# One transformer layer on one core: the opening written as one list, with the condition spread on chip and four tiles in the first batch

## The chip, the core and the metric

The kernel runs on one core of a Trainium2 chip, as one launch. The metric is the device time of that launch in microseconds (us), the median of three runs. The engines are TensorE (PE, with its weight loads PEld), VectorE (DVE), ScalarE (ACT), GpSimd (POOL) and SyncE (SP), which here only issues DMAs. Each runs its own instructions in the order in which they were written and waits on semaphores for the others.

## The reference

One encoder layer over 1024 tokens of 1024 features, float32. Cut to what the change touches:

```python
cond = jax.nn.silu(c)                                  # c: 1 x 1024
mod = cond @ w_ada[l] + b_ada[l]                       # 1024 x 6144
sh1, sc1, g1, sh2, sc2, g2 = jnp.split(mod, 6, axis=-1)
h = modulate(rms_norm(x, norm_mix_g[l]), sh1, sc1)     # norm(x)*(1+sc1)+sh1
proj = h @ w_in[l]
q_a, k_a, v_a, qk_m, v_m, o_m, gates = jnp.split(proj, splits, axis=-1)
y_attn = axial_gqa_attention(q_a, k_a, v_a, ...)       # 8 heads of 64
y_mem = bidirectional_mlstm(qk_m, v_m, o_m, gates, ...)
x = x + g1 * (concat(y_attn, y_mem) @ w_out[l])        # then the SwiGLU FFN, then a last norm
```

## The kernel before

Features lie on the 128 partitions and tokens along the free axis, so x is eight tiles `x0` to `x7` of 128 x 1024, worked in two halves `n` of 512 tokens. Every float32 product is made of three: each operand is split into a high part (fp32r) and the rest, and `mm3` (L295 to L297) adds high x high, low x high and high x low in PSUM. For the weights ACT makes the high part `whi` and POOL the low part `wlo`; for the normed input, ACT makes `hh` and POOL (for `x0` DVE) makes `hl`.

The opening does this. `cond`, the silu of c, is loaded onto all 128 partitions. ACT squares the tiles of x, DVE and POOL add them into `ssx`, and PE sums over the partitions with a matmul of ones (`ms`). DVE and ACT turn that into the reciprocal root (`sq`). A column of the modulation is one "dot": DVE multiplies a transposed column block `ada` (128 x 1024) with `cond` and sums along the free axis; each feature tile k needs two, column 8+k (scale) and column k (shift). Then for each half DVE multiplies x by the root, ACT applies scale and shift, ACT makes `hh`, and `hl` follows. PE takes each tile k as it comes, for the first batch of three tiles of output features: k, v and the first q tile, 18 matmuls for each k.

The work after that is a list of units, `IN`: `t` are chunk units (tokens on the partitions; `t0` holds v of the memory heads and the gates, eight times 24 matmuls of 272 columns), `q` the other q tiles, `f` the tiles that go through the convolution. Each q or f unit is 48 matmuls of 512 columns.

What sets the order: a class `Clock` keeps an expected time for each engine and emits each step when that model says it is ready. So one set of costs orders all five engines' instructions, and the DMAs on SP's one queue. Attention starts when the model says that the last q tile and the gates are ready; from there `un`, the stream of the units that are left, fills the gaps that the model sees in attention and then in the memory heads. The gates' rows pass through a long chain on DVE that ends in `dexp` and a small matmul (`T`, L918).

Buffers: `ada` columns share five `big` buffers, raw weight pieces three `wst` buffers.

```python
for f in range(3):
    mm3(acc0[f][n], weights(2 * f, k, 4), (h_hi[k][:, halves(n)], h_lo[k][:, halves(n)]),
        k == 0, k == KT - 1)
    ck.pe(0.65)
...
return rope_ok[3].done and gates_ok.done and not open_sum[0]      # stops the stage ahead of attention
```

Of the kernel before, what the change touches and what calls it, by code (L numbers as in the profile page):

```python
# [11 lines left out]
F32 = mybir.dt.float32  # L12
# [8 lines left out]
P = 128  # L21
# [19 lines left out]
WARM = 6  # L41
WARM0 = 9
POOLED = (0,)
# [4 lines left out]
IN = ([("t", 0), ("q", 1), ("q", 2), ("q", 3), ("f", 0), ("f", 4), ("f", 1), ("f", 5), ("t", 2), ("f", 2), ("f", 6),  # L48
# [21 lines left out]
class Flag:  # L70
    """done: what sets it is emitted; t: when that is expected to end"""
# [12 lines left out]
class Engine:  # L84
    """An engine's instructions with their expected times."""
# [39 lines left out]
class Clock:  # L125
    """Emits instructions in the order of expected times (us), each engine's in the order in which they are ready."""
# [16 lines left out]
    def chain(self, delay, *steps, flag=None, bg=None):  # L143
        """Functions that follow one another. bg: the engine of each step; the step waits until that is idle."""
# [35 lines left out]
    def need(self, *flags):  # L180
        """What sets the flags is emitted before what follows."""
# [23 lines left out]
    def streams(self, mains, fills=(), stop=None):  # L205
        """Runs streams, the first that is ready first, until the mains have ended or stop() holds."""
# [14 lines left out]
class Stream:  # L221
    """A part of the tensor engine's work: a generator that yields the flags that its next piece needs."""
# [15 lines left out]
def layer_kernel(ctx, tc, xT, c, w_ada, vecs, cons, rope, w_f, w_t0, w_t, w_o, w_gu, w_d, out):  # L238
# [8 lines left out]
    # ---------------------------------------------------------------- constants  # L247
    both = const.tile([P, 2], F32, name="both")
# [6 lines left out]
    nc.scalar.dma_start(con, cons)  # L255
# [15 lines left out]
    # DRAM scratch  # L271
# [39 lines left out]
    def psum_open(name, tags, bufs=1):  # L311
        """tags: name -> (tag, buffers)"""
# [7 lines left out]
    class slot:  # L320
        """what frees the next tile of a tag"""
# [26 lines left out]
    with tc.manual_schedule():  # L348
# [20 lines left out]
        va = kvp.tile([P, NJ, 2, P], F32R, name="va")  # L369
        k2 = [[kvp.tile([P, S], F32R, name=f"k2{i}{g}") for i in range(2)] for g in range(2)]  # L370
# [3 lines left out]
        # ---------------------------------------------------- weights in a ring of six pieces  # L374
# [33 lines left out]
        specs = conv_w(0) + conv_w(1) + conv_w(2)  # L408
# [12 lines left out]
        def raw(shape, src, flag, arrived):  # L421
            """a transfer into the ring of three; flag: it has been used; arrived(tile, delay)"""
# [10 lines left out]
        def split(p, delay, src, shape, *before, lo=None):  # L433
            """the parts of a piece"""
# [12 lines left out]
        def piece(i):  # L447
            """a piece; its transfer, where it has one of its own"""
# [11 lines left out]
        def load_piece():  # L460
            """the next piece, once there is room for it"""
# [20 lines left out]
        psum_open("ps0", {n: ("ps0", 8) for n in ("acc", "acct", "ms", "tr", "T")}, 8)  # L482

# [32 lines left out]
        for j in (8, 0):  # L516
            ada_load(j)
# [1543 lines left out]
```

## Time and profile before

| what | value |
|---|---|
| median of three runs | 1436.59 us (1433.66 to 1437.8) |
| span of the profiled execution, first to last instruction | 1431.8 us |
| PE busy | 1310.1 us, 91% |
| DVE busy | 1075.9 us, 75% |
| POOL busy | 792.6 us, 55% |
| ACT busy | 660.6 us, 46% |

The profile is of one execution. Its own time is known only as the span; the median of the timed runs is 4.8 us above that. Busy shares are over the whole span. The stages differ: in the opening DVE is the busiest engine, in attention and behind it PE is.

### The profile page before, as it was taken

The page shows a single profiled execution, that of the slowest core. Times are in us where ns is not written, and L with a number is a line of the kernel's source. Part 1 is how long each engine was busy: PE and PEld are TensorE (multiplying, and loading weights), DVE is VectorE, ACT ScalarE, POOL GpSimd, SP SyncE. Part 2 cuts the span into 40 slices and gives each one's busy share as a digit, 9 for nine tenths or more (in the row PEclk, how much of TensorE's full clock was granted, in tenths as well). Part 3 has the DMA queues.
Part 4 walks back from the last instruction along what each step waited for, and adds up shares of the span by engine and source line. Part 5 has one row for each costly group of instructions (what it writes and reads, how often), then busy time and mean ns, then how long its engine had stood idle before and what let it go on. Part 6 is the DMA issues. An engine that isn't in the chain of part 4 may idle for free.

```text
span 1431.8 us, 19550 instructions
## 1 busy us (share of the span) xinstructions
PE 1310.1 (91%) x6594; PEld 1075.7 (75%) x6602; DVE 1075.9 (75%) x1542; ACT 660.6 (46%) x1191; POOL 792.6 (55%) x624
## 2 busy tenths in 40 slices
PE   5789799999999999899877899999999999979997
PEld 2577677888878988777655688888888887757786
DVE  6947989987788836776899786766666654988676
ACT  5444326677666645454555333332333234433462
POOL 5555454444444336766557564554544444799942
PEclk9899899999999999999999999999999999999999
DMA  7446452322112144824742342232333159623324
GB/s 285 158 127 198 148 153 78 118 66 77 44 52 60 38 136 127 291 94 165 239 155 67 102 141 103 96 106 101 111 110 102 62 185 339 247 67 88 103 63 151
DMA packets 103172, 184.40 MB, mean 129 GB/s; under 512 B 11296, under 2 KB 32672, under 8 KB 103072
## 3 DMA queue, kind: packets, MB, share of 16 engines
q1 hardware_dynamic: 89968, 161.06, 35.2%
q10 hardware_dynamic: 13104, 22.10, 4.2%
q8 instruction: 52, 0.85, 0.3%
q14 instruction: 48, 0.39, 0.1%
HBM read 136.19 MB, written 43.25 MB: 125 GB/s over the span
## 4 chain that ended last, share of the span: by engine, by line
PE 55%; DVE 19%; issue 8%; DMA 7%; POOL 6%; ACT 3%; SPq 1%; DVEq 0%; POOLq 0%; ACTq 0%
PE acc L296 13%; PE acc L295 13%; PE acc L297 13%; POOL wlo L96 3%; DVE x L96 3%; DVE ada L96 3%; DVE sst L96 3%; PE av L1025 2%; DMA wst<-act_d 2%; PE T L1006 2%; DVE PT L96 2%; PE S L974 2%; DVE y L96 2%; PE acct L295 2%; PE acct L297 1%
## 5 line engine op out<-in xcount | busy, mean ns | idle before, releaser
L96 POOL TENSOR_TENSOR wlo<-wst,whi 128x512 fp32r<-128x512 f32 (+2 forms) x208 | 309.0, 1492 | 227.4 <-ACT whi L96 211.2
L96 ACT ACTIVATE whi<-wst 128x512 fp32r<-128x512 f32 (+2 forms) x219 | 131.9, 606 | 141.8 <-PE acc L297 22.4
L96 POOL TENSOR_SCALAR P<-P,sst 128x1024 f32<-128x1024 f32 x64 | 88.9, 1392 | 141.2 <-DVE sst L96 99.8
L296 PE MATMUL acc<-x,whi 128*128 128x512 f32 x352 | 139.6, 397 | 3.3 <-DVE x L96 3.3
L96 POOL TENSOR_TENSOR wlo<-wr,whi 128x512 fp32r<-128x512 f32 x60 | 83.5, 1392 | 78.3 <-ACT whi L96 74.9
L295 PE MATMUL acc<-hh,whi 128*128 128x512 f32 x224 | 97.8, 436 | 13.5 <-ACT hh L96 11.3
L297 PE MATMUL acc<-whi,wcl 128*128 128x512 f32 x244 | 98.1, 402 | 9.5 <-POOL wcl L96 9.5
L96 ACT ACTIVATE P<-S,sst,colq 128x1024 f32<-128x1024 f32 x64 | 77.3, 1207 | 52.2 <-DVE sst L96 47.8
L295 PE MATMUL acc<-whi,wch 128*128 128x512 f32 x244 | 96.8, 397 | 4.0 <-ACT wch L96 4.0
L296 PE MATMUL acc<-hl,whi 128*128 128x512 f32 x224 | 92.8, 414 | 8.2 <-POOL hl L96 4.5
L296 PE MATMUL acc<-wlo,wch 128*128 128x512 f32 x244 | 96.9, 397 | 1.1 <-POOL wlo L96 1.1
L297 PE MATMUL acc<-hh,wlo 128*128 128x512 f32 x224 | 91.5, 409 | 0.0
L96 DVE SCALAR_TENSOR_TENSOR ada<-ada,cond 128x512 f32<-128x512 f32 (+1 forms) x79 | 84.9, 1082 | 7.3 <-DMA ada<-in_w_ada_dram 7.2
L96 DVE TENSOR_TENSOR sg<-acc,sg 128x512 f32<-128x512 f32 x67 | 45.4, 687 | 59.3 <-PE acc L297 58.9
L96 ACT ACTIVATE PT<-T 128x512 fp32r<-128x512 f32 x128 | 71.4, 597 | 37.8 <-PE T L1006 37.1
L96 DVE TENSOR_TENSOR PT<-T,PT 128x512 fp32r<-128x512 f32 x128 | 82.8, 681 | 7.2 <-ACT PT L96 7.1
L96 ACT ACTIVATE whi<-wr 128x512 fp32r<-128x512 f32 x60 | 37.9, 632 | 106.1 <-DVE wr L96 49.6
L96 POOL TENSOR_TENSOR wlo<-s,whi 128x512 fp32r<-128x512 f32 x44 | 60.8, 1383 | 38.3 <-ACT whi L96 31.7
L295 PE MATMUL acct<-whi,hh 128*128 128x256 f32 (+1 forms) x256 | 79.3, 310 | 2.4 <-ACT xp L96 1.0
L296 PEld LDWEIGHTS acc<-x,whi 128*128 128x128 f32 x352 | 66.5, 189 | 19.2 <-DVE x L96 4.2
L96 DVE SCALAR_TENSOR_TENSOR x<-acc,mod,x 128x512 f32<-128x512 f32 (+1 forms) x92 | 62.7, 719 | 24.1 <-PE acc L297 24.1
L1006 PE MATMUL T<-con,P 128*128 128x128 f32 x512 | 70.2, 275 | 10.4 <-DVE PT L96 7.6
(457 smaller groups left out, 3875.1 us busy)
## 6 DMA issues: line engine op xcount, KB each, us to landing
wr<-in_w_gu_dram SPq DMA_DIRECT2D x66, 256.0 KB, 2.8
ada<-in_w_ada_dram SPq DMA_DIRECT2D x64, 256.0 KB, 3.6
wd<-in_w_d_dram SPq DMA_DIRECT2D x22, 512.0 KB, 7.0
wst<-in_w_gu_dram SPq DMA_DIRECT2D x34, 256.0 KB, 3.1
wst<-act_d SPq DMA_DIRECT2D x33, 256.0 KB, 4.1
ada<-in_w_ada_dram SPq DMA_DIRECT2D x16, 512.0 KB, 4.9
wst<-in_w_o_dram SPq DMA_DIRECT2D x32, 256.0 KB, 4.3
act_d<-sg ACTq DMA_DIRECT2D x31, 256.0 KB, 2.0
```

The source lines that it names most:

```text
L96: return fn(*args, **kw)
L295: nc.tensor.matmul(acc, w[0], x[0], start=first, stop=False)
L296: nc.tensor.matmul(acc, w[0], x[1], start=False, stop=False)
L297: nc.tensor.matmul(acc, w[1], x[0], start=False, stop=last)
L974: nc.tensor.matmul(sp[:, halves(n)], qs[:, j * P:(j + 1) * P], k2[g][m][:, halves(n)], start=m == 0, stop=m == 1)
L1006: nc.tensor.transpose(tp[:, k], Pt[q][:, (4 * b + k) * P:(4 * b + k + 1) * P], ident)
L1025: nc.tensor.matmul(av, va[:, k, h // 4], PT[it][m][:, k], start=(k, m) == (0, 0), stop=(k, m) == (NJ - 1, 1))
```

## The change

The opening is no longer emitted by the `Clock`; it is one list, with an order of its own on each engine, and the model's clock starts again at 24 us.

- c is loaded as one row (`crow`, 4 KB) into a zeroed tile. ACT takes the silu of the row, PE spreads it with a matmul of ones (`cb`), ACT copies it to `cond0`.
- The first batch is four tiles (`NT0`): k, v and two q tiles, 24 matmuls for each k. `("q", 1)` leaves `IN`.
- `con` (identity, masks) is loaded after the x tiles and the first weights, and the six DVE copies made from it come after the loop.
- Squares and their sums are whole tiles, all sums on DVE. One dot that ran on POOL and ACT (column 0) goes to DVE.
- Scale is multiplied with x and root in one DVE instruction; ACT then only adds the shift. `hl` of `x0` and of the first half of `x1` is made on DVE with the shift inside, the others stay on POOL.
- Weight pieces of the second half of the features (`first_hi(1, f)`, `first_lo(1, f)`) are split inside the loop, one for each k from 1 to 4.
- The matmuls that only keep PE busy become 12 and 4 (from 9 and 6).

```diff
-WARM = 6
-WARM0 = 9
-POOLED = (0,)
+WARM = 4
+WARM0 = 12
+NT0 = 4
-IN = ([("t", 0), ("q", 1), ("q", 2), ("q", 3), ...
+IN = ([("t", 0), ("q", 2), ("q", 3), ...
...
-    nc.scalar.dma_start(con, cons)
...
+        gp.memset(crow, 0.0)
+        nc.sync.dma_start(crow[0:1], c)
+        for k in range(KT):
+            nc.sync.dma_start(x_t[k], xT[k])
...
+        for j in (8, 0):
+            ada_load(j)
+        for f in range(NT0):
+            first_load(0, f)
+        for j in (9, 1, 10):
+            ada_load(j)
+        nc.sync.dma_start(con, cons)
+        for f in range(NT0):
+            first_load(1, f)
...
+        def dot(j):
+            ve.scalar_tensor_tensor(ada_t[j], ada_t[j], 1.0, cond0, op0=OP.mult, op1=OP.mult, accum_out=modacc[:, 0, j:j + 1])
...
+        ac.activation(crow[0:1], crow[0:1], AF.Silu)
+        ac.activation(both[:, 2:3], eps, AF.Abs_reciprocal_sqrt)
+        for n in range(NH):
+            nc.tensor.matmul(cb[n], ones, crow[:, halves(n)], start=True, stop=True)
...
+        for _ in range(WARM0):
+            nc.tensor.matmul(acc0[0][0], ones, crow[:, 0:HALF], start=True, stop=True)
...
+        def xr(k, n):
+            x = x_t[k][:, halves(n)]
+            ve.scalar_tensor_tensor(x, x, sc1[:, k:k + 1], rstd[n], op0=OP.mult, op1=OP.mult)
...
+        def h_lo_of(k, n, whole):
+            x, hi, lo = x_t[k][:, halves(n)], h_hi[k][:, halves(n)].bitcast(F32), h_lo[k][:, halves(n)]
+            if whole:
+                gp.tensor_sub(lo, x, hi)
+            else:
+                ve.scalar_tensor_tensor(lo, x, mod[:, k:k + 1], hi, op0=OP.add, op1=OP.subtract)
...
+        def prepare(k):
...
+            if k + 1 < KT:
+                if k > 1:
+                    ada_load(9 + k)
+                ada_load(k + 1)
+            dot(8 + k)
+            gain(k)
+            dot(k)
+            shift(k)
+            fast = k == 1
             for n in range(NH):
...
+                xr(k, n)
+                h_hi_of(k, n, not (fast and n == 0))
+                h_lo_of(k, n, not (fast and n == 0))
+            if k < 5:
+                first_hi(1, k - 1)
+                first_lo(1, k - 1, gp)
...
+        ck.until(24.0)
         for k in range(KT):
...
+            if k + 1 < KT:
+                prepare(k + 1)
+            seq = [(f, n, i) for n in range(NH) for f in range(NT0) for i in range(3)]
+            if k == 0:
+                seq = [(f, n, i) for n in range(NH) for i in range(3) for f in range(NT0)]
+            elif k == KT - 1:
+                seq = [(f, n, i) for f in range(NT0) for n in range(NH) for i in range(3)]
+            for f, n, i in seq:
+                mm(k, f, n, i)
+                ck.pe(0.23)
+                if n == 1 and i == 2 and (k == 3 or k == 7 and f < 2):
+                    load_piece()
...
         ck.at(2.5, lambda: rope_steps(0, [(a, Flag()) for a in acc0[2]]))
+        ck.chain(0.0, *k2_ok, lambda: rope_steps(1, [(a, Flag()) for a in acc0[3]]))
```

On POOL, in the loop over k, the low parts stood so before (`hl` is the input's, `wlo` the weights'; 128x544 are pieces of `t0`; line L96 is the helper through which the `Clock` emits):

```order
L96 TENSOR_TENSOR wlo<-wst,whi 128x512 x5
L96 TENSOR_TENSOR hl_224<-x_240,hh_216 128x512
L96 TENSOR_TENSOR wlo<-wst,whi 128x512
L96 TENSOR_TENSOR hl_224<-x_240,hh_216 128x512
L96 TENSOR_TENSOR hl_225<-x_241,hh_217 128x512 x2
```

And they stand so in the changed kernel (`spare` and `more` are places for the second pieces and their parts):

```order
L539 TENSOR_TENSOR wlo<-wst,whi 128x512 x3
L539 TENSOR_TENSOR wlo<-spare,whi 128x512
L614 TENSOR_TENSOR hl_213<-x_231,hh_205 128x512
L539 TENSOR_TENSOR wlo<-spare,whi 128x512
L614 TENSOR_TENSOR hl_214<-x_232,hh_206 128x512 x2
L539 TENSOR_TENSOR wlo<-spare,whi 128x512
L614 TENSOR_TENSOR hl_215<-x_233,hh_207 128x512 x2
L539 TENSOR_TENSOR more<-spare,more 128x512
L614 TENSOR_TENSOR hl_216<-x_234,hh_208 128x512 x2
L539 TENSOR_TENSOR more<-spare,more 128x512
L614 TENSOR_TENSOR hl_217<-x_235,hh_209 128x512 x2
L96 TENSOR_TENSOR wlo<-wst,whi 128x544 x3
```

Eight `wlo` of the first batch stand where six did, and four of them between the `hl` of the tiles.

On DVE, one tile of the loop (`x2`) stood so before, with dots of later tiles between (`sc` is the scale, `mod` the sum with the bias, `sq` the root):

```order
L96 TENSOR_TENSOR mod<-modacc,vec 128x1 x2
L96 SCALAR_TENSOR_TENSOR sc_343<-mod,vec 128x1
L96 TENSOR_TENSOR x_241<-x_241,sq 128x512
L96 SCALAR_TENSOR_TENSOR ada,modacc<-ada,cond 128x1024
L96 TENSOR_TENSOR x_241<-x_241,sq 128x512
```

It stands so in the changed kernel, each tile with its own two dots ahead of it:

```order
L542 SCALAR_TENSOR_TENSOR ada,modacc<-ada,cond 128x1024
L552 SCALAR_TENSOR_TENSOR sc_270<-modacc,b_271,vec 128x1
L542 SCALAR_TENSOR_TENSOR ada,modacc<-ada,cond 128x1024
L549 TENSOR_TENSOR mod<-modacc,vec 128x1
L600 SCALAR_TENSOR_TENSOR x_232<-x_232,sc_270,sq 128x512 x2
```

On SP's queue, the last modulation columns of the opening (the two behind the second `wst` row are columns 15 and 7) stand so in the changed kernel:

```order
L509 DMA ada<-in_w_ada_dram 128x1024 x7
L294 DMA wst<-in_w_t_dram 128x544 x3
L509 DMA ada<-in_w_ada_dram 128x1024 x2
L294 DMA wst<-in_w_t_dram 128x544
L509 DMA ada<-in_w_ada_dram 128x1024 x2
L294 DMA wst<-in_w_f_dram 128x512 x2
```

They now stand behind the fourth piece of `t0`; before, all columns stood ahead of `t0`'s pieces.

Behind the opening the order is the model's again. Counted in the order of PE's instructions: between the `T` of `dexp` and the first score matmul stand 93 matmuls of 512 columns before and 54 after; inside attention the units that fill have 279 of 512 columns and 312 of 256 before, 258 and 432 after; between attention's last instruction and the end of the units that fill, 264 of 256 columns before and 144 after. From the first units of the FFN on the order on PE is the same.

## Rows read from the trace of the kernel before

**Rows 1.** The page, its first line.
```profile
span 1431.8 us, 19550 instructions
```
**Rows 2.** Stretches: busy PE, PEld, DVE, ACT, POOL (instructions); granted clock, DMA share, GB/s.
```profile
41.20:77.20 36.00, 28.74 (x107) 21.25 (x107) 35.79 (x53) 16.16 (x24) 21.47 (x14) 0.93 0.42 130
...
89.80:118.30 28.50, 28.50 (x222) 27.54 (x221) 21.40 (x37) 10.88 (x23) 12.08 (x6) 1.00 0.48 129
118.30:177.30 59.00, 48.55 (x216) 38.83 (x214) 49.90 (x75) 25.16 (x35) 34.10 (x20) 0.90 0.56 176
177.30:206.50 29.20, 27.70 (x108) 22.26 (x109) 21.39 (x26) 6.49 (x10) 13.88 (x10) 0.86 0.58 171
206.50:507.00 300.50, 285.48 (x1873) 250.05 (x1871) 255.03 (x429) 196.54 (x343) 134.14 (x101) 1.00 0.23 67
507.00:560.00 53.00, 50.15 (x368) 47.17 (x372) 23.63 (x68) 26.60 (x76) 28.05 (x54) 1.00 0.44 137
```
**Rows 3.** DVE's instructions in order of time, in the opening.
```profile
18.89 3.43 DVE L96 TENSOR_TENSOR ssx<-ssx,sq 128x512 f32<-128x512 f32 x2
...
30.63 0.69 DVE L96 TENSOR_TENSOR x<-x,sq 128x512 f32<-128x512 f32 x1
31.23 1.22 DVE L96 SCALAR_TENSOR_TENSOR ada<-ada,cond 128x1024 f32<-128x1024 f32 x1
...
32.37 1.22 DVE L96 SCALAR_TENSOR_TENSOR ada<-ada,cond 128x1024 f32<-128x1024 f32 x1
...
41.22 2.29 DVE L96 SCALAR_TENSOR_TENSOR ada<-ada,cond 128x1024 f32<-128x1024 f32 x1
...
45.66 0.22 DVE L96 TENSOR_TENSOR mod<-modacc,vec 128x1 f32<-128x1 f32 x2
...
74.85 2.35 DVE L96 TENSOR_TENSOR x<-x,sq 128x512 f32<-128x512 f32 x2
```
**Rows 4.** POOL's instructions in order of time, in the opening.
```profile
48.28 1.30 POOL L96 TENSOR_TENSOR hl<-x,hh 128x512 fp32r<-128x512 f32 x1 [3.63 <-ACT hh L96]
...
78.65 3.75 POOL L96 TENSOR_TENSOR hl<-x,hh 128x512 fp32r<-128x512 f32 x3 [0.25 <-ACT hh L96]
```
**Rows 5.** Groups of DVE and POOL, 20.7 to 77.3 us: count, busy, mean ns.
```profile
L96 DVE SCALAR_TENSOR_TENSOR ada<-ada,cond 128x1024 f32<-128x1024 f32 x15 | 22.3, 1504 | 0.0
L96 DVE TENSOR_TENSOR x<-x,sq 128x512 f32<-128x512 f32 x16 | 15.2, 952 | 0.0
...
L96 POOL TENSOR_TENSOR hl<-x,hh 128x512 fp32r<-128x512 f32 x11 | 18.3, 1662 | 15.2 <-ACT hh L96 15.2
L96 POOL TENSOR_TENSOR wlo<-wst,whi 128x512 fp32r<-128x512 f32 x6 | 9.9, 1662 | 6.4 <-ACT whi L96 6.3
L96 POOL TENSOR_TENSOR wlo<-wst,whi 128x544 fp32r<-128x544 f32 x3 | 4.6, 1535 | 2.4 <-ACT whi L96 2.4
```
**Rows 6.** PE's matmuls in order of time, in the opening.
```profile
7.59 9.95 PE L547 MATMUL acc<-con,ones 128*128 128x512 f32 x18 [7.59 <-DMA con<-in_cons_dram]
19.62 1.13 PE L549 MATMUL ms<-ssx,ones 128*128 128x512 f32 x2 [2.08 <-DVE ssx L96]
...
41.35 0.79 PE L296 MATMUL acc<-hl,whi 128*128 128x512 f32 x1 [3.73 <-DVE hl L96]
...
49.50 0.40 PE L295 MATMUL acc<-hh,whi 128*128 128x512 f32 x1
...
54.17 0.39 PE L297 MATMUL acc<-hh,wlo 128*128 128x512 f32 x1
...
57.84 0.50 PE L296 MATMUL acc<-hl,whi 128*128 128x512 f32 x1 [1.39 <-POOL hl L96]
...
78.62 0.79 PE L295 MATMUL acc<-hh,whi 128*128 128x512 f32 x1 [4.56 <-ACT hh L96]
```
**Rows 7.** PE's matmuls, 150 to 207 us: those that PE waited for.
```profile
176.62 0.66 PE L918 MATMUL T<-dexp,ones 64*128 64x64 f32 x2 [4.09 <-DVE dexp L96]
```
**Rows 8.** Groups of PE, 177.3 to 206.5 us.
```profile
L647 PE MATMUL ms<-con,sqk 128*128 128x2 f32 x16 | 3.6, 354 | 0.0
```

More of the change, by code (lines that the diff above doesn't have):

```diff
@@ L245, in layer_kernel @@
     mid = midpool.__enter__()
-    both = const.tile([P, 2], F32, name="both")
+    both = const.tile([P, 3], F32, name="both")
     mhalf, eps = both[:, 0:1], both[:, 1:2]
@@ L359, in layer_kernel @@
         bp = PP["ada"] = big_open(5)
+        cond0 = PP["cond"] = bp.tile([P, D], F32, name="cond", bufs=1)
         def load_cond(pool):
@@ L543, in rstd_steps @@
                             lambda: dve.scalar_tensor_tensor(v, v, -0.5, ms, op0=OP.mult, op1=OP.mult), last, flag=flag)
-        acc0 = [[psum_any([P, HALF], "acc") for _ in range(NH)] for _ in range(3)]
-        for _ in range(WARM0):
-            nc.tensor.matmul(acc0[0][0], ones, con[:, 0:HALF], start=True, stop=True)
-        for n in range(NH):
-            nc.tensor.matmul(msp[n], ones, ssx[n], start=True, stop=True)
-            ck.pe(0.86)
-            rstd_ok.append(rstd_steps(msp[n], 1.0 / D, f"n{n}", lambda y, n=n: rstd.__setitem__(n, y)))
@@ L579, in layer_kernel @@
[L579 to L607 removed]
+        spare = [kvp.tile([P, S], F32, tag=f"k2{i}", name="spare") for i in range(3)]
@@ new lines, in layer_kernel, with first_hi, first_lo @@
+        W0 = {}
+        def first_hi(b, f):
+            if (b, f) in ((1, 2), (1, 3)):
+                i = 2 * (f - 2)
+                if not i:
+                    W0["more"] = kvp.tile([P, 4, 4, P], F32R, tag="va", name="more")
+                W0[b, f] = [W0["more"][:, i + j] for j in range(2)]
+            else:
+                W0[b, f] = [wp.tile([P, 4, P], F32R, tag="w" + t, name="w" + t) for t in ("hi", "lo")]
+            ac.activation(W0[b, f][0], wst_t[b, f], AF.Copy)
+        def first_lo(b, f, eng):
+            eng.tensor_sub(W0[b, f][1], wst_t[b, f], W0[b, f][0].bitcast(F32))
@@ new lines, in layer_kernel, with root_v, root_y, root_end @@
+        rv, ry = ([small() for _ in range(NH)] for _ in range(2))
+        rstd = ry
+        def root_v(n):
+            ve.tensor_scalar(rv[n], msp[n], 1.0 / D, EPS, op0=OP.mult, op1=OP.add)
+        def root_y(n):
+            ac.activation(ry[n], msp[n], AF.Abs_reciprocal_sqrt, scale=1.0 / D, bias=eps)
+        def root_end(n):
+            ve.scalar_tensor_tensor(rv[n], rv[n], -0.5, msp[n], op0=OP.mult, op1=OP.mult)
+            ve.scalar_tensor_tensor(ry[n], rv[n], 1.5, ry[n], op0=OP.add, op1=OP.mult)
@@ new lines, in h_lo_of @@
+        def h_lo_of(k, n, whole):
+            x, hi, lo = x_t[k][:, halves(n)], h_hi[k][:, halves(n)].bitcast(F32), h_lo[k][:, halves(n)]
+            if whole:
+                gp.tensor_sub(lo, x, hi)
+            else:
+                ve.scalar_tensor_tensor(lo, x, mod[:, k:k + 1], hi, op0=OP.add, op1=OP.subtract)
+        root_v(0)
+        root_y(0)
+        ac.activation(msp[0], ry[0], AF.Square)
+        dot(8)
+        gain(0)
+        first_hi(0, 0)
+        first_lo(0, 0, gp)
+        dot(0)
@@ L610, in layer_kernel @@
+        va = kvp.tile([P, NJ, 2, P], F32R, tag="va", name="va")
+        k2 = [[kvp.tile([P, S], F32R, tag=f"k2{2 * g + i}", name=f"k2{i}{g}") for i in range(2)] for g in range(2)]
+        ve.tensor_copy(selr, C("sel"))
+        ve.tensor_copy(identb, ident)
+        for i in range(2):
+            ve.tensor_copy(maskb[:, 0, i], C("maskf"))
+            ve.tensor_copy(maskb[:, 1, i], C("maskb"))
         att = {}
```

160 lines of the change are left out of this document (69 added, 91 removed).

## The prediction, on record before the changed kernel ran

> **What bounds the kernel now.** I read the busy times by stretch first, then the instructions of each engine in the opening, then the grouped counts, and last the waits of PE behind it. The profiled execution spans 1431.8 us [rows 1]; the median of the timed runs is 4.8 us above it, and I add the change of the span to that median, 1436.6.
>
> The opening, to 89.8 us, is not bound by PE: from 41.2 to 77.2 DVE is busy 35.8 of 36.0 us, PE 28.7 [rows 2]. The instructions show why DVE is so full. A dot takes 1.22 us, and one follows another after 1.14 (31.23 to 32.37); the same dot takes 2.29 where POOL's `hl` of 42.39 begins beside it, 1.07 more [rows 3]. So I count every POOL subtraction as 1.07 us taken from DVE. Together they make a ledger from 20.7 us, where the first sum over the features leaves PE [rows 6], to the last multiplication of x, at 77.2 [rows 3]:
> - the last sum of squares, to 22.3 [rows 3]: 1.5
> - 15 dots x 1.14 = 17.1 and 16 multiplications of x x 0.60 (30.63 to 31.23) = 9.6 [rows 3, 5]
> - two `hl` on DVE and six steps of the root, 512 wide, x 0.60 = 4.8; 24 tiny ones x 0.11 [rows 3] = 2.6
> - POOL: 11 + 6 + 3 = 20 subtractions [rows 5] x 1.07 = 21.4
>
> Sum 57.0, so the end would be 77.7; measured 77.2. The ledger closes, so DVE and POOL work in turns and their sum bounds the opening. PE then needs the rest: the last `hl` ends at 82.4 [rows 4], PE goes on to 89.8.
>
> Behind it, to 118.3, PE does `t0` without a gap. From 118.3 to 177.3 the gates' chain decides: PE is busy 48.6 of 59 us, DVE 49.9 [rows 2], and PE waits 4.09 us for `dexp` [rows 7]. Attention (206.5 to 507) and the memory heads' start (to 560) are PE's: busy 285.5 of 300.5 and 50.2 of 53.0 [rows 2], with the units that are left between the attention's own work.
>
> **The change part by part.** *Up to the sums.* The load of `cond` (512 KB) and of `con` leave the head of the queue, so x lands earlier, and DVE's adds no longer take turns with POOL's. But PE stands in order: two spreads and 12 warming matmuls, two instructions each, are 28 where 18 took 9.95 us [rows 6], the first of them slow; about 14 to 15 us. They start when the row of c has its silu, from about 5 us to at latest the 7.59 us at which `con` had landed before [rows 6]. So the first sum leaves PE at 20.2 to 22.5; I take 20.5. What was gained in the sums is hidden behind PE's own queue. The second sum follows at once. For x0 DVE then has two dots (2.3), six root steps (3.6), two multiplications and two `hl` (2.4), tiny ones (0.2) and four `wlo` of POOL (4.3): 12.8, to 33.3, some 8 us ahead of PE's first dense run of before, 41.35 [rows 6]. That lead isn't kept, as the next sum shows.
>
> *The loop.* The same ledger with the changed counts, from 20.5:
> - 16 dots (the one from POOL comes over) = 18.2; x 9.6, as the scale rides in the same instruction
> - three `hl` and six root steps = 5.4; 16 tiny ones = 1.8 (a third fewer)
> - POOL up to the last x: 8 `wlo` of the batch, 4 of `t0`, 11 `hl` = 23 x 1.07 = 24.6
>
> 59.6, to 80.1; about 1 us for DVE waiting on ACT's `hh` ahead of its three own `hl`. SP adds a risk: columns 15 and 7 stand behind the fourth piece of `t0`, whose buffer comes free only when POOL has split the first, about 69 us by the ledger. A column should land by 74 to 75, when DVE wants it; price 0 to 2 us. I take 81.5 for the last x, against 77.2. Then ACT's two passes and two `hl` (1.28 each, three ran in 3.75 [rows 4]) to 84.5, and 20 of the last tile's 24 matmuls at 0.2335 us (20 steps from 49.50 to 54.17 [rows 6]) = 4.7. **The opening ends at 89.2, against 89.8**: no gain in length, but with a fourth tile done. PE's own need, 24 x 0.2335 = 5.6 us for each k, stays below the 6 to 7 us that DVE and POOL need, so the extra tile is hidden there.
>
> The Trainium skill (SBUF — State Buffer, "Who interferes with whom") says that a DVE instruction with two SBUF inputs and a GpSimd one that reads SBUF shut each other out, for the whole instruction. The trace agrees on the exclusion, at 1.07 us; with the whole 1.30 of an undisturbed `hl` [rows 4] instead, the ledger of before would end at 82.3, which 77.2 refutes, and that of after 5.3 us later. All of DVE's new instructions in the loop have two SBUF inputs, so by that rule none escapes.
>
> *Behind the opening.* `t0` takes its 28.5 us. In the gates' chain DVE now has a third rotation of q inside (two 128x1024 instructions, 2.4, and tiny ones) and the start of a convolution, less one half of a dot: 3 us more, as DVE is full there. Between `dexp`'s matmul and attention PE has 54 matmuls for 93, so 39 x 0.2335 = 9.1 less, and the 16 small `ms` of 3.6 us [rows 8] stand ahead of it. Attention starts 0.6 - 3 + 9.1 + 3.6 = 10.3 us earlier, near 196.
>
> Attention then takes more filling: 21 matmuls of 512 fewer (-4.9), 120 of 256 more; these I put at half the spacing, 0.117, so +14.0. PE-bound, that is +9.1. The 120 are missing behind it: -14.0. Together 10.3 - 9.1 + 14.0 = 15.2 us earlier. The other count is that PE's work behind the opening falls by one unit, 48 x 0.2335 = 11.2, plus the 0.6: 11.8 if PE idles as long as before. The first count says that it also idles 3.4 us less. Between them I take **13**: 1423.6. The six moved DVE copies and `con`'s load lie in DVE's pause behind the last x and cost nothing; if that cover fails, under 1.5 us.
>
> **The rivals.**
> - *The opening gets shorter.* POOL's subtractions may fall into DVE's waits for ACT and cost it less. For it: the first three `wlo` of before did so in part, and the ledger is 0.5 us too long. Against: the ledger closes with all 20 counted. At half price 12 us go; then PE, from about 30 us with 8 x 5.6, would end near 77. 12 us more gain: 1411.
> - *The gain is not handed on.* DVE is busy 255 of 300.5 us in attention [rows 2]; if the memory heads' own chain sets their pace and filling there was free, the 14.0 are not given back and only 10.3 - 9.1 = 1.2 us are left: 1435.4, no change. Against: PE 50.2 of 53.0 [rows 2].
> - *Slower: PE's clock falls in the loop.* PE now waits a little at every half tile. After 1.39 us of waiting a matmul still takes 0.50, then 0.40; after 4.56 us it takes 0.79 [rows 6], and the stretch to 77.2 had a granted clock of 0.93 [rows 2], nearly all at 2.4 GHz. At 1.2 GHz a k costs 24 x 0.467 = 11.2 us and PE, not DVE, sets the pace: seven of them from 37 us (33.3, two dots, one x and ACT's pass) end at 115, 26 later, so 13 us slower: 1450. It decides once more than three or four of the seven run so ((11.2 - 6.9) x 3 = 13). Against: waits should be 1 to 2 us.
> - *The gates' chain eats the start.* A third rotation that costs 10 instead of 3 leaves attention 3 us earlier; the total is then 8 us earlier, inside the range.
>
> **How the numbers follow.** Forecast, 1417 to 1431: 0.53. Shorter opening: 0.14. Not handed on: 0.20. Clock or another longer opening: 0.13. The predicted time is the likeliest, 1423.6. Its own range is 1417 to 1431; the 8 in 10 take in most of the rivals on both sides, 1411 to 1438. About 0.3% (4.3 us) is what a measurement of this kernel can tell from no change: faster means below 1432.3, which the forecast, the shorter opening and a little of the third give, 0.69; within it 0.18; slower, above 1440.9, 0.13.
>
> **What the changed profile would show.** Right: the first sums leave PE at 20 to 22 us with no wait for DVE; the last multiplication of x near 81; the last matmul of the batch near 89; dots of 2.29 us as often as POOL subtracts; granted clock near 1 from 40 to 80; the first score matmul near 196; attention about 9 us longer, and the last chunk unit's end 12 to 15 earlier. From the FFN on every stretch has its old length. Wrong: a last x well before 75 (the turns cost less), matmuls of 0.79 us in the loop (the clock), a first score matmul at 203 or later (the gates), or an attention that grows by 15 us or more.

## The result, and the profile after

The changed kernel takes 1440.1 us (median of 13 runs, 1437.5 to 1444.7) against 1434.1 us for the kernel before, timed beside it (13 runs, 1428.3 to 1439.4): ratio 1.0043, 95% interval 1.0029 to 1.0058. It is 0.4% slower, where 13 us less was forecast. The profiled executions differ by more, by 11.1 us [rows 1]:

```profile
span 1442.9 us, 19529 instructions
```

A run's time stands 1.8 us above its span. So the profiled run of the changed kernel, at 1444.7 us, is the slowest of its 13 and 4.6 above their median, while that of before, at 1433.7, is 0.4 below its own. About 5 of the 11.1 us belong to this pair of executions and not to the change. Two runs of the experiments below, 3 and 9, have the same order on PE from `t0` on, and I set them beside.

To find where the time went I read the same few moments in the trace of PE and DVE of the kernels, and cut the execution at them. The columns are the change that the prediction's terms put on each stretch and the change that the traces show.

| stretch, by its end (before, after) | put | measured | in runs 3 and 9 |
|---|---|---|---|
| first matmul of `t0` (89.8, 92.7) | -0.6 | +3.0 | +2.6, +2.3 |
| last `gI` copy of `t0` (118.5, 126.4) | 0 | +4.9 | +4.9, +4.9 |
| `dexp`'s matmul (176.6, 189.2) | +3 | +4.7 | +5.1, +3.8 |
| first score matmul (206.8, 204.2) | -12.7 | -15.1 | -15.1, -15.1 |
| last `av` of attention (507.0, 518.9) | +9.1 | +14.5 | +12.1, +10.0 |
| first `ms` behind the memory heads (695.3, 702.6) | -14.0 | -4.6 | -5.4, -3.2 |
| end (1431.8, 1442.9) | 0 | +3.8 | +2.0, +1.4 |

The largest miss stands behind attention (9.4 us), then attention (5.4), `t0` (4.9), the rest (3.8) and the opening (3.6). Busy times by stretch of the changed kernel, with the columns of [rows 2]:

```profile
41.20:77.20 36.00, 29.55 (x117) 21.14 (x115) 34.64 (x40) 17.40 (x29) 26.72 (x16) 1.00 0.36 118
...
118.30:177.30 59.00, 50.29 (x241) 41.50 (x240) 45.93 (x58) 23.97 (x34) 41.01 (x21) 0.89 0.59 178
177.30:206.50 29.20, 23.20 (x92) 18.04 (x93) 28.75 (x44) 7.74 (x12) 11.56 (x10) 0.87 0.43 131
206.50:507.00 300.50, 285.62 (x1869) 253.34 (x1868) 248.05 (x423) 191.44 (x338) 129.98 (x99) 0.98 0.26 76
507.00:560.00 53.00, 48.69 (x357) 45.57 (x355) 28.00 (x68) 25.92 (x72) 20.99 (x40) 0.97 0.40 122
650.00:670.00 20.00, 10.76 (x59) 7.95 (x57) 15.74 (x40) 8.43 (x21) 7.48 (x7) 0.90 0.17 54
```

In the loop (to 77.2) DVE is still the full engine and PE runs at its upper clock, 1.00, as forecast. The new thing is the last row: late in the memory heads' stage PE is busy only half of the time. In the kernel before, whose attention ends 12 us earlier, the row of the stretch 12 us earlier is:

```profile
638.00:658.00 20.00, 18.80 (x99) 15.74 (x101) 16.66 (x41) 9.35 (x23) 12.55 (x10) 1.00 0.36 114
```

DVE's instructions in order of time, as in [rows 3]:

```profile
67.88 1.21 DVE L542 SCALAR_TENSOR_TENSOR ada<-ada,cond 128x1024 f32<-128x1024 f32 x1
69.02 0.08 DVE L542 DVE_READ_ACCUMULATOR ada<-ada,cond 128x1 f32 x1
69.13 1.14 DVE L552 SCALAR_TENSOR_TENSOR sc<-modacc,b,vec 128x1 f32<-128x1 f32 x1
...
78.28 1.42 DVE L542 SCALAR_TENSOR_TENSOR ada<-ada,cond 128x1024 f32<-128x1024 f32 x1 [2.08 <-DMA ada<-in_w_ada_dram]
...
83.14 1.40 DVE L600 SCALAR_TENSOR_TENSOR x<-x,sc,sq 128x512 f32<-128x512 f32 x2
...
118.40 0.46 DVE L96 COPY gI<-acct 128x16 f32<-128x16 f32 x2
124.11 2.19 DVE L96 SCALAR_TENSOR_TENSOR ada<-ada,cond 128x512 f32<-128x512 f32 x1 [5.25 <-DMA ada<-in_w_ada_dram]
126.23 0.08 DVE L96 DVE_READ_ACCUMULATOR ada<-ada,cond 128x1 f32 x1
126.23 0.16 DVE L96 COPY gI<-acct 128x16 f32<-128x16 f32 x1
```

The wait of 2.08 us for column 15 came at the top of its price (0 to 2); the last multiplication of x ends at 84.5. The last copy into `gI`, 0.16 us of work on which the whole gates' chain hangs, stands behind a late half-column (a dot over 512 columns) that waits 5.25 us for its transfer. Nothing in the prediction named it. Before, the copy stood ahead of such a wait:

```profile
118.35 0.17 DVE L96 COPY gI<-acct 128x16 f32<-128x16 f32 x1 [0.52 <-PE acct L297]
121.89 0.94 DVE L96 SCALAR_TENSOR_TENSOR ada<-ada,cond 128x512 f32<-128x512 f32 x1 [3.37 <-DMA ada<-in_w_ada_dram]
```

PE's matmuls in order of time, to set beside [rows 6, 7]:

```profile
9.13 11.32 PE L564 MATMUL acc<-crow,ones 128*128 128x512 f32 x24
20.29 1.88 PE L593 MATMUL ms<-ssx,ones 128*128 128x512 f32 x4
...
189.21 0.40 PE L1002 MATMUL T<-dexp,ones 64*128 64x64 f32 x2 [1.36 <-DVE dexp L96]
...
204.20 1.09 PE L1058 MATMUL S<-k,qs 128*128 128x512 f32 x4
...
664.66 0.66 PE L1932 MATMUL tr<-con,hs 128*128 128x128 f32 x4 [1.65 <-POOL hs L96]
671.88 0.80 PE L289 MATMUL acc<-yah,whi 128*128 128x512 f32 x1 [6.57 <-ACT yah L96]
673.24 0.80 PE L290 MATMUL acc<-yal,whi 128*128 128x512 f32 x1 [0.56 <-POOL yal L96]
```

The sums do leave PE behind its warming matmuls. At 664 us the memory heads' own matmuls are over and PE has nothing left until the last y has been stored, loaded and split: a wait of 6.57 us. Before, units of the first output product still filled that place, and its longest wait there was this:

```profile
666.42 0.65 PE L1848 MATMUL tr<-con,hs 128*128 128x128 f32 x4 [1.60 <-POOL hs L96]
```

Besides waits of under 1 us that both kernels have, the changed one also waits ahead of the first `ms` behind the memory heads, from 661 to 703 us (total, times, longest):

```profile
PE ms L1243 <- DVE ssq L96: 3.1, 1, 3.1
```

### The profile page after: what moved, and what is told of

Its sections match the earlier page's. It is cut to its first block, busy times and chain, and to the rows that moved or that the text cites. A ratio compares the mean times of both kernels' runs of the same rounds, so it can differ in the third digit from the quotient of the medians.

```text
span 1442.9 us, 19529 instructions
## 1 busy us (share of the span) xinstructions
PE 1317.8 (91%) x6608; PEld 1081.9 (75%) x6608; DVE 1085.3 (75%) x1537; ACT 653.8 (45%) x1182; POOL 780.8 (54%) x618
## 4 chain that ended last, share of the span: by engine, by line
PE 55%; DVE 25%; issue 7%; POOL 5%; ACT 4%; DMA 3%; SPq 0%; DVEq 0%; ACTq 0%; POOLq 0%
PE acc L290 13%; PE acc L289 13%; PE acc L291 13%; DVE sst L96 3%; DVE x L96 3%; PE av L1109 3%; POOL wlo L96 3%; DVE y L96 2%; PE T L1090 2%; DVE PT L96 2%; PE S L1058 2%; DVE ada L96 2%; DVE ada L542 1%; DVE x L600 1%; DVE s L96 1%
## 5 line engine op out<-in xcount | busy, mean ns | idle before, releaser
L96 POOL TENSOR_TENSOR wlo<-wst,whi 128x512 fp32r<-128x512 f32 (+2 forms) x200 | 294.3, 1478 | 203.5 <-ACT whi L96 192.5
L96 ACT ACTIVATE whi<-wst 128x512 fp32r<-128x512 f32 (+2 forms) x211 | 126.2, 605 | 122.4 <-PE acc L290 19.1
L96 POOL TENSOR_SCALAR P<-P,sst 128x1024 f32<-128x1024 f32 x64 | 88.2, 1380 | 161.1 <-DVE sst L96 132.0
L96 POOL TENSOR_TENSOR wlo<-wr,whi 128x512 fp32r<-128x512 f32 x60 | 83.7, 1396 | 81.4 <-ACT whi L96 81.4
L96 ACT ACTIVATE P<-S,sst,colq 128x1024 f32<-128x1024 f32 x64 | 77.2, 1207 | 43.2 <-DVE sst L96 35.1
L96 DVE TENSOR_TENSOR PT<-T,PT 128x512 fp32r<-128x512 f32 x128 | 83.9, 683 | 14.0 <-ACT PT L96 13.6
L96 DVE TENSOR_TENSOR sg<-acc,sg 128x512 f32<-128x512 f32 x67 | 45.4, 687 | 59.8 <-PE acc L291 59.5
L96 ACT ACTIVATE PT<-T 128x512 fp32r<-128x512 f32 x128 | 72.0, 596 | 35.8 <-PE T L1090 35.2
L96 ACT ACTIVATE whi<-wr 128x512 fp32r<-128x512 f32 x60 | 37.9, 632 | 108.2 <-DVE wr L96 51.7
L96 POOL TENSOR_TENSOR wlo<-s,whi 128x512 fp32r<-128x512 f32 x44 | 60.0, 1366 | 42.1 <-ACT whi L96 35.4
L96 DVE TENSOR_REDUCE sst<-S 128x1 f32<-128x1024 f32 x64 | 77.8, 1216 | 4.5 <-PE S L1058 4.4
L96 DVE SCALAR_TENSOR_TENSOR x<-acc,mod,x 128x512 f32<-128x512 f32 (+1 forms) x92 | 62.6, 719 | 23.2 <-PE acc L291 23.2
L1109 PE MATMUL av<-PT,va 128*128 128x256 f32 x512 | 70.5, 284 | 4.1 <-DVE PT L96 4.1
L289 PE MATMUL acc<-hh,whi 128*128 128x512 f32 x160 | 70.0, 438 | 3.3 <-ACT xp L96 3.3
L290 PE MATMUL acct<-wlo,hh 128*128 128x256 f32 (+1 forms) x256 | 72.9, 285 | 0.0
```

The lines of the kernel that those rows point to most:

```text
L96: return fn(*args, **kw)
L289: nc.tensor.matmul(acc, w[0], x[0], start=first, stop=False)
L290: nc.tensor.matmul(acc, w[0], x[1], start=False, stop=False)
L1109: nc.tensor.matmul(av, va[:, k, h // 4], PT[it][m][:, k], start=(k, m) == (0, 0), stop=(k, m) == (NJ - 1, 1))
```

## The experiments

All are edits of the changed kernel and compute the whole reference. Ratios are to the kernel before. Two runs with the same order on PE can differ by some microseconds in a stretch (shown below), so a single trace settles only larger differences.

**Run 1. Is the filling that moved into attention what costs?** The last 264 chunk matmuls are held until attention has ended.

```diff
+                           + ([att_end] if k == 0 and (ci == 3 or ci == 1 and j >= HOLD) else []))
...
         ck.streams([Stream(values()), Stream(turned()), Stream(scores())], [un])
+        att_end.set(ck, ck.t)
```

> The changed kernel, with the chunk units from t1's sixth column block on and all of t3 (264 matmuls of 256 columns) held back until attention's last instruction, so attention is filled as lightly as in the kernel before plus nothing (258 of 512 and 312 of 256 columns, instead of 258 and 432). Theory (fill costs time inside attention and is free behind it, because the memory heads' own chain sets the pace there): attention falls from 314 us to about 300, attention's end to the last y of the memory heads stays within 3 us of 159, the 6.6 us wait of PE for the last y goes down, and the total falls by 10 to 13 us, to about 1428, ratio 0.994 to 0.998. Rival 1 (PE is the bound in both stages): attention falls by 14 and the memory heads' stage grows by 14, total unchanged at 1440, ratio 1.004. Rival 2 (attention is paced by its own vector and activation chain, not by filling): attention stays near 314 and the total stays or rises, ratio 1.004 or more.

1446.0 us, ratio 1.0081 (1.0061 to 1.0101). My theory at that time fell, and its second rival held: attention does not get shorter. It takes 315.0 us with 120 chunk matmuls fewer, as long as with them (314.7), and attention's end to the first `ms` grows from 183.7 to 191.1. PE's longest wait of run 1 from 460 to 518 us (total, times, longest) shows why:

```profile
PE T L1094 <- DVE PT L97: 11.5, 9, 2.6
```

And this is its busy row from 480 to 500 us:

```profile
480.00:500.00 20.00, 14.81 (x84) 12.80 (x83) 12.82 (x23) 10.91 (x20) 4.93 (x5) 0.84 0.03 7
```

With the fill the same stretch of the changed kernel reads:

```profile
480.00:500.00 20.00, 19.47 (x151) 18.43 (x149) 14.29 (x26) 11.85 (x24) 5.53 (x5) 1.00 0.15 43
```

At attention's end the fill stood in PE's waits for `PT`; without it PE waits and its clock falls to 0.84. There the fill was free, and 14.0 us of it behind attention cost 7.4. Run 1's attention has 4.9 us of filling less than that of before (21 matmuls of 512 columns) and is still 14.8 us longer, so the count of the filling alone does not give attention's length.

**Run 2. The wait ahead of the last `gI` copy.** No late half-columns start until `t0`'s gate rows are in `gI`.

```diff
                 ck.need(*vo_ok[0])
+                gi_ok.set(ck, ck.t)
...
-            if ck.t > t_ada[0]:
+            if ck.t > t_ada[0] and gi_ok.done:
```

> The changed kernel, with no late modulation half-columns started until t0's gate rows are in gI. Theory (the gates' chain starts late because the last gI copy stands on DVE behind a dot that waits 5.25 us for its transfer): the last gI copy comes at about 121 instead of 126.2, the T of dexp near 184 instead of 189.2; by the order 33 instead of 54 matmuls of 512 columns then stand ahead of the first score matmul, so that comes near 194 to 195 instead of 204.2; in attention 30 more of 512 and 96 fewer of 256 columns (7.0 less 11.2), so 310; total some 10 to 14 us less than the changed kernel, about 1428, ratio 0.994 to 0.998. Rival (DVE is full in the gates' stage anyway, the wait only moves): dexp's T stays within 2 us of 189, first score matmul near 199, total 5 to 7 us less, ratio 0.999 to 1.001.

1434.6 us, ratio 0.9993 (0.9976 to 1.0010), 5.6 us less than the changed kernel (7 by the ratios). In DVE's order the copy now waits for PE alone:

```profile
120.65 0.17 DVE L96 COPY gI<-acct 128x16 f32<-128x16 f32 x1 [2.83 <-PE acct L291]
```

The first score matmul comes at 193.9, 10.3 earlier, as the theory had it: 4.9 from the wait, 4.3 from the 21 matmuls that then stand no longer ahead of it, and most of the rest from an opening that ended 0.7 earlier in this trace. The total gained about half of what I put: with 240 instead of 144 chunk matmuls left, the stretch behind attention grew from 183.7 to 189.7.

**Run 3. Column 15 behind `t0`'s fourth piece.** The fourth piece is issued two tiles later.

```diff
-                if n == 1 and i == 2 and (k == 3 or k == 7 and f < 2):
+                if n == 1 and i == 2 and (k == 3 and f < 3 or k == 5 and f == 3 or k == 7 and f < 2):
```

> The changed kernel, with the fourth piece of t0 issued two tiles later, behind columns 15 and 7. Theory (DVE waits 2.08 us for column 15, which stands on SP's queue behind that piece, and PE's clock then falls): the wait is gone, the last multiplication of x ends near 82 instead of 84.5, the granted clock from 77 to 90 stays near 1, the opening ends near 89.5 instead of 92.7, total 3 us less, ratio 1.002. Rival (DVE and POOL in turns set the pace, and the wait was covered, or t0 now waits for its fourth piece): opening ends within 1 us of 92.7 or t0 gets a gap, total unchanged, ratio 1.004.

1440.8 us, ratio 1.0049 (1.0031 to 1.0067): no change, as the rival had it. In DVE's order the wait is gone, but the dot now takes its turn with POOL, which had run through the wait:

```profile
76.45 2.35 DVE L542 SCALAR_TENSOR_TENSOR ada<-ada,cond 128x1024 f32<-128x1024 f32 x1
```

The last multiplication of x ends at 83.6 instead of 84.5, the opening at 92.3 instead of 92.7. In this trace the sums left PE 0.3 us later, so without the wait the way from the sums to the last x is 1.3 us shorter, not 2.1.

**Run 4. The list without the fourth tile; run 5, the same with the hold of run 2.** q1 is a unit of its own again.

```diff
-NT0 = 4
+NT0 = 3
...
-IN = ([("t", 0), ("q", 2), ("q", 3), ("f", 0), ("f", 4), ("f", 1), ("f", 5), ("t", 2), ("f", 2), ("f", 6),
+IN = ([("t", 0), ("q", 1), ("q", 2), ("q", 3), ("f", 0), ("f", 4), ("f", 1), ("f", 5), ("t", 2), ("f", 2), ("f", 6),
...
-        ck.chain(0.0, *k2_ok, lambda: rope_steps(1, [(a, Flag()) for a in acc0[3]]))
```

> The changed kernel's opening with three tiles in the first batch instead of four, q1 again as a unit of its own behind t0: the list alone, without the fourth tile. Theory (the list itself does not lengthen or shorten the opening much; the loss comes from how many fill matmuls land in attention): the opening ends 3 to 4 us earlier than with four tiles, near 89 to 90; 93 matmuls again between dexp and the first score matmul, which comes near 208 to 211; 279 of 512 and 384 of 256 columns inside attention, 72 more than the kernel before, so attention takes about 308; total 1436 to 1442, ratio 1.001 to 1.005. Rival (the fourth tile is what costs, by its low parts on POOL and its rotation in the gates' chain): total back at the kernel before or under it, ratio 0.996 to 1.000.

> The list with three tiles in the first batch, and no late modulation half-columns until t0's gate rows are in gI. With three tiles alone the last gI copy came 33.2 us behind the first matmul of t0, with the hold 28.8. Theory (the gates' chain starts late by that wait, and its end gates attention): last gI copy near 117.4, T of dexp near 171.4, first score matmul near 202, the order of PE's fill in attention unchanged (279 and 384), so every later stage 4.4 us earlier, total near 1421.6, ratio 0.990 to 0.993. Rival (the half-columns that are started later take their time in attention, where DVE is nearly full): attention grows by 3 to 5 us and the total stays near 1426, ratio 0.993 to 0.996.

Three tiles: 1426.0 us, ratio 0.9943 (0.9924 to 0.9962), below what either theory gave. That is 14 us under the changed kernel, by the fourth tile alone. Attention takes 308.2 us, as put. With the hold: 1421.2 us, ratio 0.9913 (0.9891 to 0.9936), the best version here. The forecast for the second held to the microsecond or two: last `gI` copy at 116.8, `dexp`'s matmul at 171.0, first score matmul at 200.7.

Runs 2 and 5 differ in the tile alone. From the last `gI` copy to `dexp`'s matmul they take 62.4 and 54.2 us. Groups of DVE in that stretch (count, busy, mean ns, idle ahead) of run 2, with four tiles:

```profile
L96 DVE TENSOR_TENSOR qg<-qg,sw 128x1024 f32<-128x1024 f32 x3 | 4.6, 1520 | 0.1
...
L96 DVE TENSOR_TENSOR qg<-qg,rps 128x1024 f32<-128x1024 f32 x3 | 4.5, 1486 | 0.0
...
L96 DVE TENSOR_SCALAR colq<-rqv 128x16 f32<-128x16 f32 x3 | 2.7, 896 | 2.6 <-POOL rqv L96 2.6
```

The same groups of run 5, with three:

```profile
L96 DVE TENSOR_TENSOR qg<-qg,rps 128x1024 f32<-128x1024 f32 x2 | 3.5, 1725 | 0.0
L96 DVE TENSOR_TENSOR qg<-qg,sw 128x1024 f32<-128x1024 f32 x2 | 3.2, 1616 | 0.0
L96 DVE TENSOR_SCALAR colq<-rqv 128x16 f32<-128x16 f32 x2 | 2.5, 1258 | 0.8 <-POOL rqv L96 0.8
```

These rows make 2.6 us of the 8.2 by their busy time, which is what I had put for the rotation's own work, and 1.8 by the longer wait for `rqv`. DVE's other instructions are the same in both and busy 2.6 us longer; its waits are 3.0 us longer in all, with 3.6 us for a `ms` of PE (L731) that the three tiles lack and shorter ones for transfers. So the third rotation cost 8 with the waits that came with it, near the 10 of the rival on the gates' chain and not the 3 that I took.

In the opening the fourth tile costs 4.1 us (88.6 against 92.7), of which 1.0 stands already in the sums, by the traces and not by the tile. From the sums to the last multiplication of x it is 3.3 us (3.4 between runs 2 and 5): two `wlo` make 2.1, and the wait for column 15, which no trace with three tiles has, the 1.3 of run 3. From there to the end it is -0.2 (1.4 between runs 2 and 5), so PE's own 24 matmuls a tile are hidden or nearly so.

One caution on the total: up to the first `ms` behind the memory heads the three tiles alone are level with the kernel before (695.3 both), with the hold 4.4 ahead. Another 7 us each come between there and the FFN's dense part, at whose start DVE's instructions stand in another order. So run 4's gain over the kernel before comes from there, not from the opening. No run separates that piece.

**Runs 6 to 8. The products drawn forward.** Between attention and the last `na` of the memory heads the changed kernel has 120 chunk matmuls fewer (14.0 us), but 57 more matmuls of the first output product, 201 for 144 (13.3 us; 147 if one counts to the heads' last `ni`): the planner fills the hole from behind. Runs 6 and 7 hold the last four of those units, run 8 all of them, behind the last `na`; run 7 has the hold of run 2 too.

```diff
-                yield [y[2], pieces[w0][2]] + ([slot("acc")] if k == 0 else [])
+                yield [y[2], pieces[w0][2]] + ([slot("acc")] if k == 0 else []) + (
+                    [heads[MH - 1]["back"][0]] if not mem and i >= 12 and k == 0 else [])
```

> The changed kernel, with the last four units of the first output product (those from the thirteenth on, the ones that read attention's y) held until the memory heads' last product na is given out. In the changed kernel 201 of these products' 512-column matmuls stand ahead of the last na, in the kernel before 147; here 144. Theory (up to the last na the memory heads' stage is PE's, and the 120 chunk matmuls that are missing were replaced by products drawn forward, which then lack as cover for the wait for the last y): attention's end to the last na falls from 143.0 to about 130 to 133 us (57 x 0.2335 = 13.3 less), PE's wait of 6.6 us for the last y goes away, the first sum of squares behind it comes 8 to 12 us earlier than 702.6, total near 1430, ratio 0.995 to 0.999. Rival (the memory heads' own chain sets the pace and filling there is free): the last na stays within 3 us of 662, the held products come behind it, the sum of squares stays at 702 or comes up to 13 us later, total 1440 or more, ratio 1.004 to 1.012.

> The changed kernel with both holds: no late modulation half-columns until t0's gate rows are in gI, and the last four units of the first output product behind the last na. With the first hold alone 168 products stood ahead of the last na, here 144. Theory (PE's stage up to the last na): attention's end to the last na falls from 147.6 to about 142 us (24 x 0.2335 = 5.6), the first sum of squares from 694.7 to about 689 to 692, total 1429 to 1432, ratio 0.995 to 0.998. Rival (chain of the memory heads sets the pace): last na unchanged, total 1434 or more, ratio 0.999 to 1.003.

> The changed kernel, with all units of the first output product held until the memory heads' last na is given out, so that besides its own products only the 144 chunk matmuls stand in that stage ahead of the last na; 201 matmuls of 512 columns (46.9 us of PE) are taken out from under it and come behind it. Theory (the memory heads' own chain over the vector engines sets the pace, and 57 matmuls less gave 4.5 us of 13.3): attention's end to the last na falls from 143 to no less than about 125 to 130 us, PE idles there, and the total rises by 25 us or more, ratio 1.02 or more. Rival (PE is the bound up to the last na, with some slack from the order): it falls to 100 to 110 us, and the total rises by less than 15 us, ratio under 1.015.

Run 6: 1435.6 us, ratio 1.0016 (1.0004 to 1.0029). Run 7: 1433.9, ratio 1.0001 (0.9984 to 1.0017), like run 2. Run 8: 1457.0, ratio 1.0175 (1.0153 to 1.0196). From attention's end to the last `na` the changed kernel takes 143.0 us; run 6 takes 138.5 with these 13.3 us of PE's work less, run 8 125.4 with 46.9 less. Neither of my two theories is right alone: PE's work there is worth 0.34 to 0.38 of its length. Run 8's total rose by 17 us over the changed kernel, where the theory had 25 or more. PE's waits of run 8 in that stretch (total, times, longest) name what sets the pace once PE has room:

```profile
PE ni L1872 <- DVE num L96: 6.8, 11, 2.1
PE na L1867 <- DVE W L96: 4.8, 3, 2.4
PE tr L1760 <- DVE W L96: 4.0, 4, 2.3
```

It is the heads' own chain over DVE. The granted clock is down there too: 0.84 from 560 to 600 us. In run 6 the cover is back, and PE waits for the last y only this much:

```profile
670.08 0.50 PE L289 MATMUL acc<-yah,whi 128*128 128x512 f32 x1 [0.83 <-ACT ymt L96]
```

**Runs 9 to 11. Fewer warming matmuls.** 4 ahead of the sums instead of 12 (run 9), the same on the best version (run 10), and with all three repairs on four tiles (run 11).

```diff
-WARM0 = 12
+WARM0 = 4
```

> The changed kernel with 4 warming matmuls ahead of the sums instead of 12. Theory (PE's own queue of warming matmuls holds the sums: DVE waited 2.5 us for them while the squares were summed at 18.9): the sums leave PE near 19.9 instead of 21.3, every step of the opening 1.4 us earlier, its end near 91.3, total 1.4 us less, ratio 1.003. Rival (the warming keeps PE's clock up): the first matmuls of the batch run at 0.79 instead of 0.40 us, or the sums themselves are slow, and the opening ends at 92.7 or later, ratio 1.004 or more.

> The list with three tiles, the hold of the late half-columns until t0's gate rows are in gI, and 4 warming matmuls instead of 12. Theory: the sums leave PE up to 1.4 us earlier and each later stage with them, total 1420 to 1421, ratio 0.990 to 0.992. Rival (gains of the opening are lost again in the order behind it): total 1421 to 1424, ratio 0.991 to 0.994.

> The changed kernel with four tiles and three repairs: the hold of the late half-columns until gI, t0's fourth piece behind columns 15 and 7, and 4 warming matmuls. Theory (the fourth tile costs 8 us in the gates' chain by its rotation and 4 in the opening, and gives one unit back, of which the memory heads' stage hands on a third): opening ends near 91.3, total 1431 to 1433, ratio 0.998 to 1.000, not under the three-tile version. Rival (the repairs are all that the four tiles lacked): total 1421 to 1424, ratio 0.991 to 0.994.

Run 9: 1438.7 us, ratio 1.0036 (1.0021 to 1.0051). Its sums start at 18.5 instead of 20.3, but the opening ends only 0.7 earlier. After the shorter warming PE waits, and the sums' four matmuls take 3.78 us where the changed kernel's took 1.88, so that the second sum leaves PE no earlier, at 22.3 for 22.2:

```profile
18.50 3.78 PE L593 MATMUL ms<-ssx,ones 128*128 128x512 f32 x4 [5.46 <-DVE ssx L578]
```

The rival's slow sums came. Run 10: 1422.9, ratio 0.9933 (0.9914 to 0.9953), no gain over run 5. Run 11: 1437.3, ratio 1.0024 (1.0010 to 1.0038): the repairs do not bring four tiles under three, nor to the 1431 to 1433 that I put. There the last multiplication of x ends 2.1 us earlier than in the changed kernel, and yet the opening ends at 92.6. PE's matmuls of run 11 in order of time:

```profile
75.15 0.50 PE L668 MATMUL acc<-hh,whi 128*128 128x512 f32 x1
78.90 0.80 PE L668 MATMUL acc<-hl,whi 128*128 128x512 f32 x1 [3.25 <-POOL hl L614]
79.49 0.63 PE L668 MATMUL acc<-hh,wlo 128*128 128x512 f32 x1
79.92 0.63 PE L668 MATMUL acc<-hh,whi 128*128 128x512 f32 x1
...
84.61 0.48 PE L668 MATMUL acc<-hh,wlo 128*128 128x512 f32 x1
84.93 0.40 PE L668 MATMUL acc<-hh,whi 128*128 128x512 f32 x1
```

Its busy row from 77 to 85 us, with the granted clock as third from the end:

```profile
77.00:85.00 8.00, 6.10 (x15) 4.82 (x16) 6.15 (x14) 3.09 (x5) 5.83 (x4) 0.57 0.48 165
```

After the wait of 3.25 us for POOL the matmuls of tile 6 start every 0.43 us, which is the lower clock of 1.2 GHz, until 84.6, and from there PE works without a gap to the end. With four tiles PE has no room for that: the clock rival, refuted in the loop, holds for its end. In the changed kernel it cost nothing yet: there too matmuls start every 0.43 us from 79.4 to 82.3, behind a wait of 2.29 us for `hl`, with a granted clock of 0.77 from 77.2 to 84.5, but PE then waits twice more for `hl` (0.66 and 0.31 us).

## Why the prediction was wrong, step by step

**The step that failed** is "The 120 are missing behind it: -14.0". It rested on "Attention (206.5 to 507) and the memory heads' start (to 560) are PE's", read from 50.2 busy us of 53.0 [rows 2], the first third of a stage of 160. The 14.0 us were not handed back: the planner drew 13.3 us of other products into the hole, so the last `na` came as late after attention as before (143.0 and 143.2). Behind it PE then had 13.3 us less to do, but the wait of 6.57 us for the last y, that of 3.1 us for the sums of squares, and matmuls at the lower clock (granted 0.88 from 661.6 to 702.6, before 0.99 from 650 to 695.3) took two thirds of that. Measured -4.6. The rival "the gain is not handed on" had the place right, but filling there is not free as it said: it is worth a little over a third of its length (run 8: 17.6 of 46.9).

**The gates' start** "t0 takes its 28.5 us" held for PE (run 2: 28.8 to the last copy), but the chain hangs on a DVE copy, and the prediction, which named what stands behind a waiting transfer for column 15, did not look at the late half-columns in that way: 4.9 us, shown by run 2.

**The gates' chain**, 3 put: the rotation's own work was sized right at 2.6, the waits and the longer instructions that come with it were put at nothing, "as DVE is full there", where it was busy 49.9 of 59 us [rows 2]; 8.2 in all between runs 2 and 5. The prediction's own sign for it, a first score matmul at 203 or later, came (204.2). Against the kernel before it shows only as 4.7, since with three tiles this stretch takes 54.2 us where it took 58.1 before; what fell away there stays open.

**The opening.** Last x put at 81.5, measured 84.5: 0.8 from the sums (21.3 for 20.5), 0.8 from DVE's three waits for `hh` (1.8 for about 1), and from column 15 0.9 (1.3 by run 3, of which 0.4 was taken), all named ahead; half a us is left. The ledger held: the loop's period is 7.03 us a tile against the 6.9 put. The end came 3.5 late, 3.0 of it by the last x. "The extra tile is hidden there" holds for PE's matmuls; the tile's cost, 3.3 us ahead of the last x, is the two `wlo`, which stood in the sum, and column 15's wait, which stood there as a risk. In the rival of the shorter opening, 30 us and 8 x 5.6 make 75, not 77; nothing hangs on it.

**dexp to the first score**: the count of 54 matmuls was right, -15.1 measured for -12.7.

**Attention**, +9.1 put, +14.5 measured. Run 9, with the same order on PE, takes 310.2 us where the changed kernel takes 314.7: +10.0, so the term was right in size. What PE doesn't work in attention stayed the same (15.0 us of 300.2 before, 13.9 of 310.2 in run 9), which fits a stage bound by PE; but run 1 shows that this is not so at attention's end, so that the count came out so near is partly luck. The other 4.5 us, 2.9 of PE's busy time and 1.6 of waiting, go with PE's clock at its start: the changed kernel has 0.91 and 0.96 in the first two stretches of 40 us, run 9 0.96 and 1.00, and before it was 1.00 [rows 2]. The busy rows of the changed kernel there:

```profile
204.20:244.20 40.00, 34.21 (x169) 27.96 (x168) 32.97 (x55) 19.77 (x34) 15.25 (x12) 0.91 0.32 101
244.20:284.20 40.00, 37.58 (x269) 34.97 (x268) 36.61 (x63) 23.67 (x44) 17.32 (x10) 0.96 0.34 99
```

And those of run 9:

```profile
202.62:242.62 40.00, 34.20 (x175) 27.73 (x174) 34.09 (x57) 21.15 (x35) 15.72 (x13) 0.96 0.33 103
242.62:282.62 40.00, 38.99 (x292) 35.87 (x290) 37.29 (x69) 25.48 (x46) 17.56 (x11) 1.00 0.36 109
```

The order of the instructions is the same; the third column from the end, the clock, is not. Over the whole of attention the changed kernel and run 9 read:

```profile
204.20:518.90 314.70, 299.18 (x1971) 265.92 (x1969) 257.43 (x438) 198.24 (x350) 132.89 (x101) 0.98 0.25 73
202.60:512.80 310.20, 296.32 (x1971) 262.87 (x1969) 255.04 (x438) 198.58 (x350) 132.53 (x101) 0.99 0.25 74
```

What lowers the clock in one execution and not in the other, no run shows.

**"From the FFN on every stretch has its old length"** was wrong by 3.8 us in this trace, by 2.0 and 1.4 in runs 3 and 9. The order on PE is the same there, but DVE's differs at the FFN's start, where DVE is full. What of it is that order and what the clock stays open.

## What to carry to other kernels

Work that a planner uses as filling has a different price in each stage; measure that price by taking filling out, and look at what the planner draws into the hole, before counting a moved unit as a gain. Read a stage over its whole length, above all its last wait, not over a stretch where the engine happens to be full. A short instruction that starts a long chain must not stand on its engine behind one that waits for a transfer: taking one such wait away gave about 5 us with four tiles and with three alike, by the medians.

## What the runs showed of the hardware

- A wait can cost PE more than its length. In run 11, behind 3.25 us of waiting, 13 matmuls started every 0.43 us instead of 0.2335; where filling was taken out (runs 1 and 8) PE waited and the granted clock fell to 0.84. How much of the gain that stayed out is the clock, and how much the chain that PE waits for, was not separated. The Trainium skill (TensorE: Matmul & The Clock Gate, "HAM oscillation — how this bites in real kernels") describes a kernel in which waits between bursts bring the lower clock back each time; the matmuls behind the wait agree.
- The same order on PE took 310.2, 312.3, 313.6, 314.6 and 314.7 us for attention in five traces (runs 9, 3, 6, 8 and the changed kernel). The granted clock of the first two stretches of 40 us was 0.96 and 1.00 in the first two, 0.96 and 0.96 in the third, 0.91 and 0.96 in the last two.
- The turn that DVE loses to POOL falls on whatever stands there, however small: `sc`, one element a partition, takes 1.10 to 1.14 us beside a subtraction of POOL and 0.22 without. The Trainium skill (SBUF — State Buffer, "Who interferes with whom") has a DVE instruction with two SBUF inputs shut out while GpSimd reads, and names no size below which it escapes; the trace agrees.
